# A hybrid-heads encoder kernel: one pipeline for the D, A, B and C attention groups, issued on TensorE in written order, with the attention constants loaded at the start

## The chip, the cores and the metric

The kernel runs on one core of a Trainium2 chip. The metric is the device time of one execution in microseconds (us). The time before is the median of 3 runs, 3581.33 us (3578.38 to 3583.49). PE is TensorE, the matmul engine, and PEld its weight loads; DVE is VectorE, ACT ScalarE, POOL GpSimd, and SP the queue that issues most DMAs.

## The reference

Two layers of an encoder trunk work on 2048 tokens of 1024 channels in float32. A layer is a normalisation, one input projection whose columns belong to four groups of attention heads, a SiLU gate on each group's output, one output projection and a residual add.

```python
for l in range(DEPTH):                      # 2 layers
    z = rmsnorm(x, norm_g[l]) @ w_in[l]     # q, k, v, gate of A, B, C, D
    o_a = dense attention, 4 query heads on 2 key heads, q and k normalised, rotary
    o_b = sliding window of 128 to each side, rotary, a sink logit in the softmax
    o_c = 2-D neighbourhood (8 x 16) with a relative position bias
    o_d = (softmax(q1 k1) - lam * softmax(q2 k2)) @ v, then a norm   # dense, head halves of 32
    x = x + concat(o_a * silu(g_a), ..., o_d * silu(g_d)) @ w_out[l]
out = rmsnorm(x, final_g)
```

lam is a scalar of the layer, made from four small vectors; the sink is one number for each head of B.

## The kernel before

Tokens are handled in 16 tiles of 128. Projections are done with a split of each operand into two float32r parts (three matmuls for each product); scores and outputs of the attention run in float32r or as float32 transposes. A layer goes through four stages.

**1. Projection of D.** For each tile, x is transposed and split (`make_ht`), the D columns are projected, and queries and keys are rotated, transposed and stored. Half of the transposed tiles stay in SBUF, the others go to DRAM.

**2. The D phase.** 32 units (2 key heads x 16 query tiles). A unit computes four passes of scores, 2048 keys each, in four matmuls of 512 columns (L490); DVE moves every score bank to SBUF and takes its maximum (L491); ACT makes the exponential of 2048 columns (L498); DVE combines the two softmaxes of a head (`comb`, L715). Then come eight *fronts*: four 128 x 128 transposes into one PSUM bank (L507) and an evacuation by `evac` (L468 on ACT or L466 on DVE, chosen by the unit's list `ev`, which is empty for D: ACT). Then the *O block*: 32 matmuls with the values (L514). Then the finish `fin_d`, a generator that is advanced once a slot: evacuation, squares, a small matmul (L584), a reciprocal root on POOL (L114), the gate on POOL (L538), a transpose (L543) and the product (L546), which is stored.

Beside it runs the *filler*: the input projection of groups A, B and C, 20 chunks of 8 tiles, each tile (`z`, L315 to L319) 24 matmuls of 256 columns into a PSUM buffer of the pool `zps2` (two buffers), followed by its post-processing. Query chunks (A, B and C: 48 of the 160 tiles) later call `q_store` or `qc_store`, which transpose the finished queries into a `zps2` buffer as well (L754, L798) and evacuate with ACT and DVE (L757, L758); they are called from inside a later tile, after its sixth of eight k steps (`KQ = 5`). In a query chunk of A the rotation and the norm are on POOL (L745, L329, L337, L114, L748).

**3. The A, B and C phase.** 32 groups of three units: one dense A unit and two B units, and in the second half two C units instead. Queries, keys and bias tables are loaded by `prep`; small key tables are built by `k_build` from inside the loop.

**4. Output projection** (L218), during which the next layer's D weights are loaded.

The order in stages 2 and 3 is written out by `drive`. It walks the units; beside a unit's fronts (and, in D, two gap slots ahead of them) it advances the generator of the *next* unit's scores, so that they end with the last front; a *slot* is one such step, and each slot also advances the filler by `FR2 = 12.2` matmuls. Ahead of the first unit it gives half that to each of its 16 score steps.

What this order means differs. Before, the D phase's `drive` call is a plain program: the framework's scheduler takes the written order as a priority, and orders each engine's instructions by its own model of time, so PE may be given a later filler where an earlier instruction isn't ready in that model. Only stage 3's call lies in `tc.manual_schedule(engines={PE})`, where PE's instructions stay in the order in which they are written. On the other engines the scheduler sets the order in both. Between the two calls the pools of stage 2 are closed, the rest of the filler is written out, and stage 3's first loads and first key build are made.

`layer_consts` loads a layer's small tensors, among them `snk` (the sinks), `nsnk` (their negative, by DVE) and `nlam`; the tiles lie in a pool with one buffer, so layer 1's load of a tile waits for layer 0's last reader. It is called once for each layer, ahead of stage 1's loop.

`build_rep` makes C's bias table in DRAM, with POOL copies in a pool of its own (`bb`). It is called by the filler at its seventh chunk.

Of the kernel before, what the change touches and what calls it, by code (L numbers as in the profile page):

```python
# [20 lines left out]
S = 2048  # L21
# [52 lines left out]
def trunk_kernel(ctx, tc, x, norm_g, w_in, w_out, qn_a, kn_a, sink_b, rpb_c, lam_q1, lam_k1, lam_q2, lam_k2,  # L74
# [44 lines left out]
    def build_rep(l, pool):  # L119
        rep = dr.tile([64, 60, 40], F32, name=f"rep{l}")  # L120
        rr = pool.tile([60, 31], F32, name="rraw")
        nc.sync.dma_start(out=rr, in_=rpb_c[l].rearrange("h a b -> (h a) b"))
        G.tensor_scalar(rr, rr, 8.0, 0.0, op0=ALU.mult, op1=ALU.add)
        rint = pool.tile([60, 64], F32, name="rint")
# [7 lines left out]
        for c0, n in ((0, 4), (4, 4), (57, 4), (61, 3)):  # L132
            re = pool.tile([60, 4, 40], F32, tag="redge", name="redge")
# [120 lines left out]

    for l in range(depth):
# [5 lines left out]
        snk = lay.tile([128, 4], F32, tag="snk", name="snk")  # L261
        nsnk = lay.tile([128, 4], F32, tag="nsnk", name="nsnk")
# [4 lines left out]
        nlam = lay.tile([128, 1], F32, tag="nlam", name="nlam")  # L267

        def layer_consts():
# [4 lines left out]
            nc.sync.dma_start(out=snk, in_=sink_b[l].partition_broadcast(128))  # L274
            V.tensor_scalar(nsnk, snk, -1.0, 0.0, op0=ALU.mult, op1=ALU.add)
            for i, a in enumerate((lam_q1, lam_q2, lam_k1, lam_k2)):
                nc.sync.dma_start(out=lv[:, i, :], in_=a[l].partition_broadcast(128))
            V.tensor_tensor(lp, lv[:, 0:2, :], lv[:, 2:4, :], op=ALU.mult)
            V.tensor_reduce(ls, lp, axis=AX.X, op=ALU.add)
            A.activation(le, ls, ACTF.Exp)  # L280
            V.tensor_tensor(nlam, le[:, 1:2], le[:, 0:1], op=ALU.subtract)
            V.tensor_scalar(nlam, nlam, lam_init, 0.0, op0=ALU.subtract, op1=ALU.add)
# [65 lines left out]
        with tc.tile_pool(name="wd", bufs=16, reuse_waits="tile") as wp, tc.tile_pool(name="st", bufs=3, reuse_waits="tile") as st:  # L348
# [107 lines left out]
        with tc.tile_pool(name="sm", bufs=6, reuse_waits="tile") as sm, \  # L456
# [60 lines left out]
            def small_front(u, i):  # L517
                ws, n, kw = u["ws"], u["n"], u.get("kw", 128)
                js = [j for j in (2 * i, 2 * i + 1) if j < n]
                if i == 0:  # L520
                    u["pt"] = u["ptp"].tile([128, 1024], F32, tag="pt", name="PT")
# [55 lines left out]
            def fin_d(u):  # L577
# [3 lines left out]
                yield  # L581
                yield
# [9 lines left out]
                yield  # L592
                yield
                yield
# [124 lines left out]
            with tc.tile_pool(name="st2", bufs=5, reuse_waits="tile") as st, tc.tile_pool(name="w2", bufs=10, reuse_waits="tile") as wp, \  # L719
                    tc.tile_pool(name="z2", bufs=2, reuse_waits="tile") as zp, tc.tile_pool(name="zps2", bufs=2, space=PSUM, reuse_waits="tile") as zps:  # L720
# [129 lines left out]
                def filler():  # L850
# [46 lines left out]
                with tc.tile_pool(name="bb", bufs=1, reuse_waits="tile") as bbp, tc.tile_pool(name="p1", bufs=1, reuse_waits="tile") as p1p:  # L897
                    kds = {(0, 0): kd0[0], (0, 1): kd0[1]}

                    def get_kd(kv):  # L900
                        def f(c):
                            if (kv, c) not in kds:
# [6 lines left out]
                                  p1=p1p, fixed=False, front=dense_front, back=dense_back, get_o=own_o,  # L909
# [283 lines left out]
```

## Time and profile before

| | us |
|---|---|
| median of 3 runs | 3581.33 |
| lowest, highest | 3578.38, 3583.49 |
| the profiled execution | 3577.66 |
| its span, first to last instruction | 3575.9 |
| PE busy in it | 3440.1 |
| DVE busy | 2501.2 |
| ACT busy | 2111.0 |
| POOL busy | 954.5 |
| D phase of layer 0, first score to last O block | 178.4 to 1081 |
| D phase of layer 1 | 1949.6 to 2856 |
| first A O block, layer 0 and 1 | 1095.9 and 2872.9 |

A row of a windows table gives a stretch in us from the span's start and its length, then for each engine the busy time and the number of instructions, the clock that PE was granted as a share of full speed, the share of the DMA engines and GB/s. A row of the timeline gives start and duration, the engine, the line, the operation with its output and inputs, shape and count, and in brackets how long the engine stood idle before it and what ended that. Matmuls are pipelined, so their busy times overlap: how fast PE goes is seen in the distance of starts, or in the number of matmuls in a stretch, not in busy time. A few matmul records are missing or lie on a window's edge, so counts are off by one or two.

### The profile page before, as it was taken

How to read it: one execution, taken by the hardware profiler on the slowest of the kernel's cores; microseconds unless marked ns; L12 is line 12 of the kernel's file. 1: busy time of each engine (PE TensorE's matmuls, PEld its weight loads, DVE VectorE, ACT ScalarE, POOL GpSimd, SP SyncE). 2: the span in 40 equal slices, each digit the busy share in tenths (PEclk: the TensorE clock that was granted, in tenths of full speed). 3: DMA queues.
4: the chain of work that ended last, by engine and by line, in shares of the span. 5: the costliest groups of instructions: out<-in, count | busy, mean ns of one | idle time of the engine just before them, and what ended most of it. 6: DMA issues, size and time to landing. Idle time of an engine off the chain costs nothing. (4 is left out here: it accounts for less than half of the span.)

```text
span 3575.9 us, 71599 instructions
## 1 busy us (share of the span) xinstructions
PE 3440.1 (96%) x25232; PEld 2967.9 (83%) x25232; DVE 2501.2 (70%) x7827; ACT 2111.0 (59%) x3963; POOL 954.5 (27%) x1604
## 2 busy tenths in 40 slices
PE   8989999999989999999999899999999899999999
PEld 8979898888967877877899798988889578778787
DVE  4387877777877887773233878787787778777733
ACT  4455666556667877771144556665666678777711
POOL 4455333552200001001044553256431000010000
PEclk9999999999999999999999999999999999999999
DMA  4542325332233354335445323253331332543243
GB/s 147 187 113 86 79 84 163 93 93 77 70 93 87 83 126 123 90 99 174 146 130 183 99 79 91 70 179 90 81 86 58 96 85 85 136 114 98 89 159 112
DMA packets 355777, 387.47 MB, mean 108 GB/s; under 512 B 59802, under 2 KB 298586, under 8 KB 350298
## 3 DMA queue, kind: packets, MB, share of 16 engines
q1 hardware_dynamic: 351098, 367.17, 35.3%
q10 hardware_dynamic: 4320, 15.73, 1.3%
q8 instruction: 199, 3.26, 0.4%
q14 instruction: 160, 1.31, 0.1%
HBM read 258.83 MB, written 123.91 MB: 107 GB/s over the span
## 5 line engine op out<-in xcount | busy, mean ns | idle before, releaser
L491 DVE TENSOR_SCALAR_CACHE_REDUCE P<-S 128x512 f32<-128x512 f32 x1536 | 1025.6, 685 | 263.6 <-PE S L490 195.2
L315 PE MATMUL z<-wt,ht 128*128 128x256 f32 (+1 forms) x3008 | 890.8, 297 | 8.9 <-ACT wt L306 4.2
L317 PE MATMUL z<-wt,ht 128*128 128x256 f32 (+1 forms) x3008 | 883.8, 294 | 2.7 <-DVE wt L309 2.7
L319 PE MATMUL z<-wt,ht 128*128 128x256 f32 (+1 forms) x3008 | 882.9, 294 | 0.0
L507 PE MATMUL PTp<-idr,P 128*128 128x128 f32 x4096 | 627.5, 276 | 40.9 <-ACT P L468 18.5
L468 ACT COPY P<-PTp 128x512 f32<-128x512 f32 x896 | 511.4, 585 | 220.0 <-PE PTp L507 215.7
L498 ACT ACTIVATE P<-P,nm 128x2048 f32<-128x2048 f32 x256 | 513.9, 2008 | 182.7 <-DVE jk L497 173.9
L507 PEld LDWEIGHTS PTp<-idr,P 128*128 128x128 f32 x4096 | 491.2, 142 | 139.0 <-ACT P L468 25.7
L315 PEld LDWEIGHTS z<-wt,ht 128*128 128x128 f32 x3008 | 569.0, 190 | 28.0 <-POOL wt L308 5.0
L317 PEld LDWEIGHTS z<-wt,ht 128*128 128x128 f32 x3008 | 569.4, 189 | 16.9 <-DVE wt L309 5.2
L319 PEld LDWEIGHTS z<-wt,ht 128*128 128x128 f32 x3008 | 569.2, 189 | 7.0
L490 PE MATMUL S<-kA,q 128*128 128x512 f32 x1024 | 362.7, 437 | 0.0
L218 PE MATMUL y<-wot,ms 128*128 128x512 f32 x1440 | 330.8, 392 | 0.0
L218 PEld LDWEIGHTS y<-wot,ms 128*128 128x128 f32 x1440 | 270.8, 188 | 59.7
L538 POOL TENSOR_TENSOR gg<-gt,rzh 128x128 f32<-128x128 f32 x192 | 76.8, 401 | 894.9 <-PE O L543 351.6
L308 POOL TENSOR_SCALAR wt<-wst,g 128x256 fp32r<-128x256 f32 (+1 forms) x336 | 213.8, 647 | 355.8 <-PE z L319 261.8
L715 DVE SCALAR_TENSOR_TENSOR P<-P,cf,P 128x2048 f32<-128x2048 f32 x128 | 306.4, 2394 | 2.7
L498 ACT ACTIVATE P<-P,nm,rr_a 128x2048 f32<-128x2048 f32 x128 | 268.5, 2098 | 63.1 <-DVE jk L497 60.7
L514 PE MATMUL O<-P,vd 128*64 128x256 f32 x2048 | 242.6, 389 | 0.6 <-ACT P L468 0.6
L514 PE MATMUL O<-P,vA 128*64 128x256 f32 x2048 | 235.1, 382 | 0.0
L490 PE MATMUL S<-kdt,qd 128*128 128x512 f32 x512 | 214.6, 440 | 8.2 <-DVE P L491 5.4
L490 PE MATMUL S<-kd,qd 128*128 128x512 f32 x512 | 208.8, 429 | 12.5 <-DVE P L491 10.9
(195 smaller groups left out, 5120.5 us busy)
## 6 DMA issues: line engine op xcount, KB each, us to landing
wst<-in_w_in_dram SPq DMA_DIRECT2D x320, 128.0 KB
qd<-qd SPq DMA_DIRECT2D x128, 128.0 KB
htd<-ht SPq DMA_DIRECT2D x16, 1024.0 KB
ht<-htd SPq DMA_DIRECT2D x16, 1024.0 KB
q<-qsA SPq DMA_DIRECT2D x128, 128.0 KB
q<-qsB SPq DMA_DIRECT2D x64, 256.0 KB
q<-qc SPq DMA_DIRECT2D x64, 256.0 KB
mload<-mx ACTq DMA_DIRECT2D x30, 512.0 KB
```

What stands on the lines that cost most here:

```text
L218: PE.matmul(ys[c], lhsT=ms[:, a, kc], rhs=wts[k][:, b, c * 512:(c + 1) * 512], start=(k == 0 and i == 0), stop=(k == KD - 1 and i == 2))
L308: G.tensor_scalar(wt[:, 0, :], s, g8[:, k:k + 1], 0.0, op0=ALU.mult, op1=ALU.add)
L315: PE.matmul(z, lhsT=h[:, 0, kc], rhs=wk[:, 0, :], start=(k == 0), stop=False)
L317: PE.matmul(z, lhsT=h[:, 0, kc], rhs=wk[:, 1, :], start=False, stop=False)
L319: PE.matmul(z, lhsT=h[:, 1, kc], rhs=wk[:, 0, :], start=False, stop=(k == KD - 1))
L468: A.copy(dst, src)
L490: PE.matmul(s, lhsT=q, rhs=k_ap[:, c:c + 512], start=(i == 0), stop=(i == len(q_list) - 1))
L491: V.tensor_scalar(p[:, c:c + 512], s, 1.0, None, op0=ALU.mult, op1=ALU.max, accum_out=mx[:, j:j + 1])
L498: A.activation(p, p, ACTF.Exp, bias=nm, scale=scale, accum_out=zacc)
L507: PE.transpose(tp[:, (h * 2 + a) * 128:(h * 2 + a + 1) * 128], p[:, h, j * 128:(j + 1) * 128], idn)
L514: PE.matmul(u["o"][a * 64:(a + 1) * 64, 0:256], lhsT=u["v"](0, j), rhs=u["p"][:, :, j * 128:(j + 1) * 128], start=(n < 2), stop=(n >= NT - 2))
L715: V.scalar_tensor_tensor(p0, p1, cf, p0, op0=ALU.mult, op1=ALU.add)
```

## The change

Both `drive` calls become one, over the 32 D units and the 32 groups of A, B and C, inside one `manual_schedule` for PE: the D phase is now also issued on PE in written order, filler included. The first A unit's scores are preceded by `switch`, which writes out what is left of the filler, closes stage 2's pools, opens stage 3's and makes its first loads; three empty steps follow it. So the first A, B scores are written beside the last D unit's fronts. The first key build of B becomes one of the queued builds, run in the last D unit. The last two D units take their finish's buffer from the same pool as the others, and wait three and five slots in place of two and three. The gap is a property of a unit.

The sink and lam constants of both layers get tiles of their own and are made by `attn_consts`, called once, in layer 0, behind `layer_consts`. `build_rep` gets one buffer out of the rotation of the query chunks (`qs`, three buffers) in place of its own pool, and puts its three tables in parts of it.

"Evacuations by slot" in the change's name has no line of its own in the diff: the lists `ev` are as before.

```diff
-    def build_rep(l, pool):
+    def build_rep(l, buf):
-        rr = pool.tile([60, 31], F32, name="rraw")
+        rr = buf[0:60, 0:31]
-        rint = pool.tile([60, 64], F32, name="rint")
+        rint = buf[0:60, 32:96]
-            re = pool.tile([60, 4, 40], F32, tag="redge", name="redge")
+            re = buf[0:60, 96:256].rearrange("p (c e) -> p c e", e=40)
...
+    snks = [const.tile([128, 4], F32, name=f"snk{m}") for m in range(depth)]
+    nsnks = [const.tile([128, 4], F32, name=f"nsnk{m}") for m in range(depth)]
+    nlams = [const.tile([128, 1], F32, name=f"nlam{m}") for m in range(depth)]
...
-            nc.sync.dma_start(out=snk, in_=sink_b[l].partition_broadcast(128))
-            V.tensor_scalar(nsnk, snk, -1.0, 0.0, op0=ALU.mult, op1=ALU.add)
...
+        def attn_consts():
+            for m in range(depth):
+                nc.sync.dma_start(out=snks[m], in_=sink_b[m].partition_broadcast(128))
+                V.tensor_scalar(nsnks[m], snks[m], -1.0, 0.0, op0=ALU.mult, op1=ALU.add)
+                for i, a in enumerate((lam_q1, lam_q2, lam_k1, lam_k2)):
+                    nc.sync.dma_start(out=lv[:, i, :], in_=a[m].partition_broadcast(128))
+                V.tensor_tensor(lp, lv[:, 0:2, :], lv[:, 2:4, :], op=ALU.mult)
+                V.tensor_reduce(ls, lp, axis=AX.X, op=ALU.add)
+                A.activation(le, ls, ACTF.Exp)
...
             if l == 0:
                 load_wd()
                 layer_consts()
+                attn_consts()
                 nc.sync.dma_start(out=bm, in_=bmask)
...
-            def drive(groups, gap, fill, f_rate, extra=None):
+            def drive(groups, fill, f_rate, extra):
                 fins = []
+                k3 = len(units_d)
...
+                    gap = g[0].get("gap", 0)
...
-                            if extra:
-                                extra(step[0])
-                            step[0] += 1
+                            if k >= k3 - 1:
+                                extra(step[0] if k >= k3 else f - 10)
+                            if k >= k3:
+                                step[0] += 1
...
                         if i == 6:
-                            build_rep(l, bbp)
+                            build_rep(l, zp.tile([128, 256], F32, tag="qs", name="rbuf", bufs=3))
...
                     for u in units[-2:]:
-                        u["fp"] = lambda: zps.tile([128, 256], F32, tag="z", name="fin")
-                    drive([[u] for u in units], GAP2, fill, FR2)
-                for _ in fill:
-                    pass
-                for f in pend_all:
-                    f()
-                for _ in side:
-                    pass
+                        u["f1"], u["f2"] = 3, 5
+                    units_d = [[u] for u in units]
...
+            def switch():
+                nonlocal tpool
+                for _ in fill:
+                    pass
+                for f in pend_all:
+                    f()
+                for _ in side:
+                    pass
+                flush()
+                ph2.close()
+                for nm, bufs in (("qst", 2), ("ql", 2), ("cb", 1), ("px", 4), ("pt", 2)):
+                    X[nm] = ph3.enter_context(tc.tile_pool(name=nm, bufs=bufs, reuse_waits="tile"))
+                for nm in ("ops2", "tps3"):
+                    X[nm] = ph3.enter_context(tc.tile_pool(name=nm, bufs=1, space=PSUM, reuse_waits="tile"))
+                tpool = cycle([tps, tps, X["tps3"]])
+                bint[1] = X["cb"].tile([128, 4, 480], F32, name="bint1")
+                cm["pool"] = X["cb"]
+                prep(0, 0)
+                kt["B"] = [big.tile([128, S], F32R, tag="b", name=f"kB{i}") for i in range(2)]
+                builds.extend(("B", 0, [e]) for e in k_load(X["ql"], "B", 0))
                 load_v("A")
-                kt["B"] = [big.tile([128, S], F32R, tag="b", name=f"kB{i}") for i in range(2)]
-                k_build("B", 0, k_load(ql, "B", 0))
                 load_v("B")
...
+                def a_first(u):
+                    switch()
+                    for _ in range(3):
+                        yield
+                    yield from a_scores(u)
...
-                with tc.manual_schedule(engines={mybir.EngineType.PE}):
-                    drive([units[i:i + 3] for i in range(0, len(units), 3)], GAP3, iter(()), 0, ex3)
+                first = units[0]
+                first["ns"] += 3
+                first["s"] = a_first
+                order = ExitStack()
+                order.enter_context(tc.manual_schedule(engines={mybir.EngineType.PE}))
+                drive(units_d + [units[i:i + 3] for i in range(0, len(units), 3)], fill, FR2, ex3)
+                order.close()
+                ph3.close()
```

More of the change, by code (lines that the diff above doesn't have):

```diff
@@ L260, in trunk_kernel @@
         sub = lay.tile([128, 64], F32, tag="sub", name="sub")
-        snk = lay.tile([128, 4], F32, tag="snk", name="snk")
-        nsnk = lay.tile([128, 4], F32, tag="nsnk", name="nsnk")
+        snk, nsnk, nlam = snks[l], nsnks[l], nlams[l]
         lv = lay.tile([128, 4, 32], F32, tag="lv", name="lv")
@@ L266, in trunk_kernel @@
         le = lay.tile([128, 2], F32, tag="le", name="le")
-        nlam = lay.tile([128, 1], F32, tag="nlam", name="nlam")
         def layer_consts():
@@ L273, in layer_consts @@
             G.tensor_scalar(sub, sub, 0.5 * (1.0 - lam_init), 0.0, op0=ALU.mult, op1=ALU.add)
[L274 to L282, printed above, removed]
+        def attn_consts():
[7 more added lines that the diff above has]
+                A.activation(le, ls, ACTF.Exp)
+                V.tensor_tensor(nlams[m], le[:, 1:2], le[:, 0:1], op=ALU.subtract)
+                V.tensor_scalar(nlams[m], nlams[m], 0.8 - 0.6 * math.exp(-0.3 * m), 0.0, op0=ALU.subtract, op1=ALU.add)
         if l > 0:
@@ L580, in fin_d @@
                 A.activation(sq, os, ACTF.Square)
-                yield
-                yield
+                for _ in range(u.get("f1", 2)):
+                    yield
                 tp = u["fp"]()
@@ L591, in fin_d @@
                 gg = finish(u["g"], rr)
-                yield
-                yield
-                yield
+                for _ in range(u.get("f2", 3)):
+                    yield
                 finish2(gg, os, u["t"], u["fb"], u["o"], u["fp"])
@@ L717, in d_scores @@
                     yield
-            with tc.tile_pool(name="st2", bufs=5, reuse_waits="tile") as st, tc.tile_pool(name="w2", bufs=10, reuse_waits="tile") as wp, \
-                    tc.tile_pool(name="z2", bufs=2, reuse_waits="tile") as zp, tc.tile_pool(name="zps2", bufs=2, space=PSUM, reuse_waits="tile") as zps:
+            if True:
+                ph2 = ExitStack()
+                st = ph2.enter_context(tc.tile_pool(name="st2", bufs=5, reuse_waits="tile"))
+                wp = ph2.enter_context(tc.tile_pool(name="w2", bufs=10, reuse_waits="tile"))
+                zp = ph2.enter_context(tc.tile_pool(name="z2", bufs=2, reuse_waits="tile"))
+                zps = ph2.enter_context(tc.tile_pool(name="zps2", bufs=2, space=PSUM, reuse_waits="tile"))
                 def sumsq_heads(z, rs, H):
@@ L896, in trunk_kernel @@
                 fill = filler()
-                with tc.tile_pool(name="bb", bufs=1, reuse_waits="tile") as bbp, tc.tile_pool(name="p1", bufs=1, reuse_waits="tile") as p1p:
+                p1p = ph2.enter_context(tc.tile_pool(name="p1", bufs=1, reuse_waits="tile"))
+                if True:
                     kds = {(0, 0): kd0[0], (0, 1): kd0[1]}
@@ L1058, in pair_o @@
                 if u["kv"] == 0:
-                    o_bc.append(ops2.tile([128, 512], F32, tag="o", name="Obc"))
+                    o_bc.append(X["ops2"].tile([128, 512], F32, tag="o", name="Obc"))
                 u["o"] = o_bc[-1]
             o_bc = []
-            def small_unit(sc, i, t, q, px, fb, ns, nv, bias=None, pre=lambda: None):
-                return dict(kv=i, t=t, s=sc, par=False, ev=(0, 1) if i else (), ns=ns, nv=nv, fin=fin_plain, fb=fb, q=q, pp=px, bias=bias, pre=pre,
-                            front=small_front, back=small_back, get_o=pair_o, oc=128 * i, ptp=ptp, fd=5 + 2 * i)
@@ L1068, in trunk_kernel, with small_unit @@
-            with tc.tile_pool(name="qst", bufs=2, reuse_waits="tile") as qst, tc.tile_pool(name="ql", bufs=2, reuse_waits="tile") as ql, \
-                    tc.tile_pool(name="cb", bufs=1, reuse_waits="tile") as cb, tc.tile_pool(name="px", bufs=4, reuse_waits="tile") as px, \
-                    tc.tile_pool(name="pt", bufs=2, reuse_waits="tile") as ptp, \
-                    tc.tile_pool(name="ops2", bufs=1, space=PSUM, reuse_waits="tile") as ops2, \
-                    tc.tile_pool(name="tps3", bufs=1, space=PSUM, reuse_waits="tile") as tps3:
-                tpool = cycle([tps, tps, tps3])
+            def small_unit(sc, i, t, q, fb, ns, nv, bias=None, pre=lambda: None):
+                return dict(kv=i, t=t, s=sc, par=False, ev=(0, 1) if i else (), ns=ns, nv=nv, fin=fin_plain, fb=fb, q=q, bias=bias, pre=pre,
+                            front=small_front, back=small_back, get_o=pair_o, oc=128 * i, fd=5 + 2 * i)
@@ new lines, in trunk_kernel @@
+            X, ph3 = {}, ExitStack()
+            loaded, builds = [], []
+            bint = [None, None]
+            cc_, edge = {}, {}
+            cm, qq = {}, {}
+            def switch():
[18 more added lines that the diff above has]
+                builds.extend(("B", 0, [e]) for e in k_load(X["ql"], "B", 0))
@@ L1074, in trunk_kernel @@
                 load_v("A")
[L1075 to L1076 removed]
                 load_v("B")
[L1078 to L1082 removed]
+            if True:
                 def prep(ps, t):
@@ L1146, in ex3 @@
                         k_build(*builds.pop(0))
-                    if step == WOU:
+                    if step == WOU and not wo_tiles:
                         for k in range(KD):
```

33 lines of the change are left out of this document (14 added, 19 removed).

## The prediction

> **What bounds the kernel now.** I read the page's first part, then a table of windows by stage, then the same kind of table for single units of the D phase, then the timeline where TensorE (PE) stands still.
>
> ```profile
> span 3575.9 us, 71599 instructions
> PE 3440.1 (96%) x25232; PEld 2967.9 (83%) x25232; DVE 2501.2 (70%) x7827; ACT 2111.0 (59%) x3963; POOL 954.5 (27%) x1604
> ```
>
> PE is busy for 96% of the span, but busy time is not speed: the windows by stage show how many matmuls it gets through. For layer 0 they are the start of the D phase (178 to 236), the stretch with filler (236 to 1008) and the stretch after the filler has run out (1008 to 1096); the last two again for layer 1.
>
> ```profile
> core 0: us, PE busy (x) PEld busy (x) DVE busy (x) ACT busy (x) POOL busy (x), PEclk, DMA share, GB/s
> 178.00:236.00 58.00, 46.72 (x299) 41.77 (x301) 49.34 (x142) 28.14 (x49) 46.67 (x81) 0.88 0.49 128
> 236.00:1008.00 772.00, 762.53 (x6006) 686.74 (x6003) 606.03 (x1829) 465.35 (x807) 296.12 (x490) 1.00 0.32 91
> 1008.00:1096.00 88.00, 69.43 (x407) 46.52 (x407) 68.63 (x241) 58.54 (x95) 9.04 (x15) 0.94 0.37 102
> 2009.00:2782.00 773.00, 764.24 (x6007) 688.47 (x6007) 606.48 (x1829) 465.34 (x807) 294.98 (x491) 1.00 0.32 91
> 2782.00:2873.00 91.00, 74.84 (x407) 49.47 (x407) 69.05 (x241) 58.62 (x95) 9.04 (x15) 0.89 0.35 98
> ```
>
> With filler PE does 6006 matmuls in 772 us, 7.8 a microsecond, and waits 9.5 us in all. After the filler it does 407 in 88 us, 4.6 a microsecond, in both layers. There VectorE (DVE) and ScalarE (ACT) set the pace, through a chain of waits. So PE bounds the filled part, the other two the tail, and where the filler ends matters.
>
> The next two tables hold windows from one unit's O block to the next, first for the filler line L319 alone (a third of the filler), then for everything.
>
> ```profile
> 830.72:855.22 24.50, 9.21 (x33) 6.21 (x33) 1.00 0.34 91
> 969.78:1000.01 30.23, 14.96 (x54) 9.99 (x53) 1.00 0.18 49
> 1000.01:1019.22 19.21, 3.08 (x11) 2.07 (x11) 1.00 0.52 137
> ```
>
> ```profile
> 830.72:855.22 24.50, 24.16 (x187) 21.06 (x186) 21.51 (x67) 15.03 (x30) 6.84 (x14) 1.00 0.34 91
> 969.78:1000.01 30.23, 30.23 (x245) 27.97 (x244) 23.30 (x68) 18.87 (x33) 3.84 (x7) 1.00 0.18 49
> 1019.22:1039.08 19.86, 14.92 (x83) 8.61 (x82) 16.58 (x54) 13.16 (x19) 1.10 (x2) 1.00 0.45 99
> 1039.08:1060.77 21.69, 17.43 (x87) 11.57 (x86) 18.30 (x59) 13.16 (x19) 1.10 (x2) 0.81 0.23 73
> 2793.24:2814.46 21.22, 17.16 (x83) 10.83 (x82) 16.91 (x54) 13.20 (x19) 1.10 (x2) 0.83 0.38 82
> 2814.46:2834.68 20.22, 16.86 (x87) 9.83 (x86) 17.58 (x58) 13.26 (x19) 1.10 (x2) 0.92 0.23 73
> ```
>
> A unit with 33 x 3 = 99 fillers takes 24.50 us, one with 54 x 3 = 162 takes 30.23: 0.091 us for each more. The scheduler gives out filler unevenly and ahead of the written rate, and three units and three quarters of a fourth are left nearly without.
>
> **Part 1: filler at its written rate.** The written order spends 98 fillers beside unit 0's scores and 122 (10 slots of 12.2) beside each unit's fronts. 3840 (160 tiles of 24) last for (3840 - 98) / 122 = 30.67 of 32 units, so 1.33 stay without, against 3.74 now (the windows after 1019.22, 1039.08 and 1060.77, and 1 - 33/122 of the one at 1000.01). A unit with 122 fillers takes 24.50 + 23 x 0.091 = 26.6 us. What PE needs for it without them comes from the pace of issue:
>
> ```profile
> 982.07 0.60 PE L507 MATMUL PTp<-idr,P 128*128 128x128 f32 x4
> 982.42 0.47 PE L490 MATMUL S<-kdt,qd 128*128 128x512 f32 x1
> 982.73 0.28 PE L319 MATMUL z<-wt,ht 128*128 128x256 f32 x1
> 982.85 0.28 PE L315 MATMUL z<-wt,ht 128*128 128x256 f32 x1
> ```
>
> Start to start a filler takes 0.12 us, four transposes 0.35, a score about 0.3 behind a transpose. 26.6 - 122 x 0.12 = 12.0 us. The four unfilled units above took 20.75 us on average, so each wastes 8.75. With 2.4 fewer in each layer the change removes 2.4 x 8.75 = 21 us, 42 in both. Moving filler between filled units is free, as their pace is linear. The scores of the first A unit lie beside the tail in both orders.
>
> **Part 2: constants.** In layer 0, where group B ends and C begins:
>
> ```profile
> 1335.57 4.00 SPq L274 DMA_DIRECT2D snk<-in_sink_b_dram  x1
> ```
>
> ```profile
> 1347.28 0.17 DVE L275 TENSOR_SCALAR nsnk<-snk 128x4 f32<-128x4 f32 x1 [9.14 <-DMA snk<-in_sink_b_dram]
> ```
>
> ```profile
> 1348.11 0.97 PE L1036 MATMUL Sc<-kC,q 128*128 128x360 f32 x2 [7.99 <-DVE P L491]
> ```
>
> Layer 1's nsnk is queued on DVE behind a load that could not start before layer 0 had read the old snk; DVE stands 9.14 us, PE 7.99 behind it. With a tile for each layer, loaded at the start, this wait goes: -8. What is late next there is PE's own work; I take nothing back. In exchange one more load chain and its DVE steps lie in the opening. The second lv set is read early in the program already, so what is new is snk, nsnk and nlam of one layer. Between 0 and one more DMA wait; DVE waited 1.88 us on the first snk:
>
> ```profile
> 21.48 0.17 DVE L275 TENSOR_SCALAR nsnk<-snk 128x4 f32<-128x4 f32 x1 [1.88 <-DMA snk<-in_sink_b_dram]
> ```
>
> I take 2.
>
> **Part 3: waits that the written order adds.** PE can no longer step past an instruction that isn't ready; behind it queue every score, transpose and filler, and DVE and ACT wait for those. Most steps have cover: the stretch of A and B units, issued in written order already, lost 0.31 us of 50 and then 0.76.
>
> ```profile
> 1100.00:1150.00 50.00, 49.69 (x411) 40.24 (x406) 41.02 (x156) 40.26 (x89) 3.60 (x9) 1.00 0.30 83
> 1150.00:1200.00 50.00, 49.24 (x405) 40.11 (x404) 41.65 (x156) 40.33 (x85) 3.61 (x9) 1.00 0.35 93
> ```
>
> That is 1% or less, as the filled stretch loses now, so I charge nothing for it. One step has little cover. The input-projection tiles z and the transposed queries qT share two PSUM buffers. In a query chunk (48 of 160 tiles) qT is transposed six fillers before the tile's end, and the next tile takes the buffer that ACT (L757) and DVE (L758) must have emptied, or z's own. The cover is six fillers and about one score: 6 x 0.12 + 0.4 = 1.1 us. I paired the 66 transposes on record with the DVE subtraction that ends each. The shortest pair, the middle one and a long one:
>
> ```profile
> 361.81 0.38 PE L754 MATMUL qT<-idr,qs 128*128 128x128 f32 x2
> 397.11 0.38 PE L754 MATMUL qT<-idr,qs 128*128 128x128 f32 x2
> 390.15 0.38 PE L754 MATMUL qT<-idr,qs 128*128 128x128 f32 x2
> ```
>
> ```profile
> 362.64 0.42 DVE L758 TENSOR_TENSOR qt<-qT,qt 128x256 fp32r<-128x256 f32 x1 [0.65 <-ACT qt L757]
> 399.33 0.40 DVE L758 TENSOR_TENSOR qt<-qT,qt 128x256 fp32r<-128x256 f32 x1
> 395.07 0.41 DVE L758 TENSOR_TENSOR qt<-qT,qt 128x256 fp32r<-128x256 f32 x1
> ```
>
> They hold the buffer for 1.25, 2.62 and 5.33 us: 0.15 us uncovered at the short end, 1.5 in the middle. About 80 tiles of both layers meet this in the steady part (the first eight of a layer lie in the start). 12 us or 120: I take 0.3 us a tile, 24 in all, nearer the short end, because a waiting PE sends no new scores and both engines empty their queues, and because z's own buffer is a second way out.
>
> In the start, PE waits now for POOL's query chain, and POOL for weights:
>
> ```profile
> 201.07 0.69 PE L754 MATMUL qT<-idr,qs 128*128 128x128 f32 x2 [4.90 <-POOL qs L748]
> ```
>
> ```profile
> 188.65 0.48 POOL L308 TENSOR_SCALAR wt<-wst,g 128x256 fp32r<-128x256 f32 x1 [5.36 <-DMA wst<-in_w_in_dram]
> ```
>
> The written order meets tile 0's last weights after 24 fillers and four scores, where the scheduler ran tile 1's filler instead: up to 5 us worse in a layer. build_rep now takes its buffer from the query rotation, so its POOL steps and loads leave this stretch: up to 4 us better. I take 0. The query and key loads at the switch are issued, as now, right after the last filler, with the unfilled third of a unit, an O block and two slots as cover; without it one load's wait would show, once in a layer.
>
> **The sum.** Against the profiled execution, 3577.66 us (span 3575.9): -42 - 8 + 2 + 24 = -24, so 3554. The median of the three runs, 3581.33, lies 3.7 above that execution; on the median's footing I forecast 3557. A difference of 0.2%, 7 us, is about what a measurement of this kernel can tell from none.
>
> **A page weighed.** In the window at 1039.08 the granted clock is 0.81, and PE's longest wait there is:
>
> ```profile
> 1045.55 0.44 PE L507 MATMUL PTp<-idr,P 128*128 128x128 f32 x2 [1.91 <-DVE P L715]
> ```
>
> The Trainium skill, "TensorE: Matmul & The Clock Gate", section "Part 1: The HAM clock gate", lets the clock fall only after an idle window of about 3.4 us; by it new waits of 0.3 or 1.5 us cost themselves alone. The trace does not agree: waits under 2 us came with 0.81. If the 80 query tiles, 5.2 us each (26.6 x 24/122), ran at 0.81, that would add 80 x 5.2 x 0.19 = 79 us. I leave it out of the sum, as the A and B stretch with its short waits shows 1.00, and keep it for the upper end.
>
> **Rivals.** *Slower: the shared PSUM buffers decide.* If the middle pair holds, 80 x 1.5 = 120 us are lost against 48 gained: +72, 3653 on the median's footing. It decides from 0.6 us a tile (48 / 80). For it: the middle and the long pairs, and DVE and ACT are busy for 79% and 60% of the filled stretch. Against it: the short pairs, and the scheduler's order itself kept running through these chunks.
>
> *No change: the first front waits.* Front 0 needs the combination of both heads, and in written order it comes two slots after the O block, 24.4 x 0.12 + 3.2 x 0.3 = 3.9 us. One of the late ones:
>
> ```profile
> 803.86 3.67 PE L514 MATMUL O<-P,vd 128*64 128x256 f32 x32
> ```
>
> ```profile
> 808.84 2.35 DVE L715 SCALAR_TENSOR_TENSOR P<-P,cf,P 128x2048 f32<-128x2048 f32 x1
> ```
>
> The block's issue ends 3.6 us after its start, the combination 3.7 us later: just covered. If DVE is 0.4 us later in each of some 60 units, 24 us go and with them the gain: about 3581. For this case also speaks that "evacuations by slot" has no line in the diff: the lists that choose DVE or ACT are the same, so that part does nothing.
>
> *Better still:* if the 9.5 and 8.8 us that PE waits in the filled stretches go too and the query tiles cost 0.15, the sum is -54, 3527.
>
> **How the numbers follow.** The forecast's case, 3535 to 3574: 0.53. Better still: 0.05. No change: 0.15. Slower: 0.27. So faster 0.58, same 0.15, slower 0.27. The range runs from 3515 to 3610; above it lie query tiles that cost over about 0.95 us each, roughly half of the slower case.
>
> **What would show it.** Right: 122 fillers in every D window but the last two, D units at 26 to 27 us, filler lasting to about 30 us before the last D block, no wait at nsnk, and the C phase and output projection unchanged. Wrong: PE waits at L315 behind ACT L757, L739 or DVE L758 summing to over 24 us a layer, waits at L507 behind L715, or D units of 28 us with 122 fillers.

## The result, and the profile after

| | time, us | against before |
|---|---|---|
| before | 3579.86, median of 4 runs (3576.71 to 3583.49) | |
| after | 3638.76, median of 4 runs (3633.92 to 3641.12) | 1.0158, 95% interval 1.0145 to 1.0171 |

The change makes the kernel 59 us slower by the medians, 57 by the ratio; the forecast was 3557, at most 3610. The first lines of the page of the changed kernel:

```profile
span 3632.1 us, 71548 instructions
PE 3431.5 (94%) x25232; PEld 2980.2 (82%) x25232; DVE 2508.2 (69%) x7827; ACT 2127.3 (59%) x3963; POOL 928.8 (26%) x1604
```

The span grew by 56.2 us, and PE's busy time fell by 8.6: the work is the same, the waiting grew. To see where, the D phase of layer 0 of the changed kernel from O block to O block, as in the prediction (columns: window, its length, then busy time and instructions of each engine, PE's clock, the DMA engines' share, GB/s). A unit without queries, three with query chunks (groups B, B and C), and the last two units:

```profile
core 0: us, PE busy (x) PEld busy (x) DVE busy (x) ACT busy (x) POOL busy (x), PEclk, DMA share, GB/s
272.40:298.50 26.10, 26.10 (x209) 23.65 (x207) 21.75 (x67) 16.01 (x27) 8.31 (x16) 1.00 0.27 77
378.10:409.70 31.60, 28.22 (x218) 24.99 (x217) 20.75 (x63) 17.62 (x30) 15.63 (x26) 1.00 0.26 65
409.70:441.80 32.10, 28.24 (x216) 24.93 (x215) 24.52 (x70) 17.69 (x32) 8.52 (x13) 1.00 0.30 80
441.80:481.60 39.80, 29.21 (x218) 25.40 (x217) 23.73 (x73) 17.62 (x35) 11.00 (x31) 0.98 0.36 88
...
1069.40:1092.40 23.00, 21.89 (x167) 18.92 (x166) 18.05 (x55) 14.14 (x25) 1.10 (x2) 1.00 0.23 80
1092.40:1113.20 20.80, 14.96 (x95) 11.35 (x95) 14.94 (x54) 14.63 (x22) 3.65 (x4) 0.92 1.06 275
```

All 29 units between the start and the last two hold 122 fillers. Those without queries take 25.9 to 27.9 us and PE stands 1.5 us in them at most; the last two are the only short ones, as forecast. Of the nine with query tiles, the two that hold B's second query chunk take only 27.3 and 27.9 us; the other seven take 30.8 to 39.8 us, and PE stands 3.4, 3.9 and 10.6 us in the three shown. What PE waits for, in the changed kernel's waits (engine, line and who ended the wait: us in all, times, longest):

```profile
PE z L320 <- DVE qt L770: 20.4, 22, 1.7
...
PE z L320 <- ACT qs L802: 13.9, 18, 1.5
PE z L320 <- POOL wt L313: 13.8, 4, 5.8
...
PE PTp L513 <- DVE P L723: 11.7, 4, 3.7
...
PE z L320 <- ACT zkv L778: 10.9, 8, 2.5
PE qT L810 <- DVE qc L819: 10.2, 4, 3.5
...
PE z L320 <- ACT zq L751: 8.9, 12, 1.2
PE z L320 <- ACT sq L736: 7.6, 5, 2.3
```

L320 is a tile's first projection matmul (L315 before). It waits for the buffer that the previous qT held (DVE qt) and for the one that the previous z held (ACT qs, zkv, zq, sq). L810 is the transposing of C's queries into their own qT. These six rows sum to 72 us in both layers. The prediction had named two of them as the sign that it is wrong, DVE qt and ACT zq (L758 and L739 before), above 24 us a layer: these two come to 29 us in both layers, so that sign by itself didn't show, while its other one, D units above 28 us with 122 fillers, did. The whole stretch from the first D score to the first A unit's O block took 917.5 and 923.3 us before in the two layers and takes 942.8 and 950.5 after, so +52.5 in all. The first D score itself comes 5.8 us later (184.2 against 178.4), and the stretch from the first A unit's O block to the first C score is 5.8 shorter (246.4 against 252.2).

### The profile page after: what moved, and what is told of

Same layout as the page of the kernel before. It is cut to its first block, busy times and chain, and to the rows that moved or that the text cites. A ratio compares the mean times of both kernels' runs of the same rounds, so it can differ in the third digit from the quotient of the medians.

```text
span 3632.1 us, 71548 instructions
## 1 busy us (share of the span) xinstructions
PE 3431.5 (94%) x25232; PEld 2980.2 (82%) x25232; DVE 2508.2 (69%) x7827; ACT 2127.3 (59%) x3963; POOL 928.8 (26%) x1604
## 4 chain that ended last, share of the span: by engine, by line
PE 74%; DVE 10%; DMA 5%; issue 4%; ACT 4%; POOL 2%; SPq 1%; POOLq 0%; DVEq 0%; ACTq 0%
PE S L496 10%; PE O L520 10%; PE y L218 10%; PE PTp L513 10%; PE z L320 9%; PE z L322 8%; PE z L324 8%; DVE P L497 4%; PE Obc L539 2%; PE PTp L531 2%; DVE P L723 2%; ACT P L504 2%; DMA wst<-in_w_in_dram 2%; PE Sc L1043 1%; DVE wt L314 1%
## 5 line engine op out<-in xcount | busy, mean ns | idle before, releaser
L497 DVE TENSOR_SCALAR_CACHE_REDUCE P<-S 128x512 f32<-128x512 f32 x1536 | 1038.6, 686 | 226.4 <-PE S L496 219.2
L320 PE MATMUL z<-wt,ht 128*128 128x256 f32 (+1 forms) x3008 | 896.8, 298 | 80.5 <-DVE qt L770 14.1
L474 ACT COPY P<-PTp 128x512 f32<-128x512 f32 x896 | 520.6, 585 | 351.7 <-PE PTp L513 347.2
L320 PEld LDWEIGHTS z<-wt,ht 128*128 128x128 f32 x3008 | 569.9, 189 | 112.5 <-ACT qs L802 19.3
L313 POOL TENSOR_SCALAR wt<-wst,g 128x256 fp32r<-128x256 f32 (+1 forms) x336 | 195.1, 591 | 450.7 <-PE z L324 332.4
L496 PE MATMUL S<-kdt,qd 128*128 128x512 f32 x512 | 229.3, 448 | 11.6 <-DVE P L497 11.4
L496 PE MATMUL S<-kd,qd 128*128 128x512 f32 x512 | 228.2, 446 | 4.5 <-DVE P L497 4.5
```

The source lines that it names most:

```text
L313: G.tensor_scalar(wt[:, 0, :], s, g8[:, k:k + 1], 0.0, op0=ALU.mult, op1=ALU.add)
L320: PE.matmul(z, lhsT=h[:, 0, kc], rhs=wk[:, 0, :], start=(k == 0), stop=False)
L474: A.copy(dst, src)
L496: PE.matmul(s, lhsT=q, rhs=k_ap[:, c:c + 512], start=(i == 0), stop=(i == len(q_list) - 1))
L497: V.tensor_scalar(p[:, c:c + 512], s, 1.0, None, op0=ALU.mult, op1=ALU.max, accum_out=mx[:, j:j + 1])
```

## Experiments

Theory: the written order turns the two PSUM buffers that z and qT share into waits. Rivals: the constants, the merged pipeline, or DVE and ACT being late whatever the buffers. Ratios are to the kernel before on the same chip. A difference of two ratios is multiplied by 3582 to give us; by the two intervals such a difference is uncertain by 5 to 8 us.

| run | median us | ratio, 95% interval |
|---|---|---|
| e6_order | 3635.72 | 1.0149 (1.0134 to 1.0164) |
| e3_noorder | 3581.65 | 0.9999 (0.9989 to 1.0008) |
| e2_consts | 3585.32 | 1.0010 (1.0000 to 1.0019) |
| e1_half | 3592.21 | 1.0028 (1.0017 to 1.0040) |
| e7_side | 3584.72 | 1.0000 (0.9991 to 1.0010) |
| e8_casts | 3551.93 | 0.9908 (0.9893 to 0.9923) |
| e9_late | 3548.76 | 0.9899 (0.9884 to 0.9914) |
| e10_nolate | 3569.89 | 0.9956 (0.9941 to 0.9971) |
| f1_aftercasts | 3612.66 | 1.0083 (1.0067 to 1.0100) |
| f2_beforecasts | 3591.02 | 1.0025 (1.0015 to 1.0035) |
| f3_actw | 3539.96 | 0.9881 (0.9866 to 0.9895) |
| f4_actstart | 3536.27 | 0.9866 (0.9850 to 0.9883) |
| g1_twotiles | 3568.39 | 0.9970 (0.9955 to 0.9984) |
| g2_mendnoorder | 3576.24 | 0.9988 (0.9979 to 0.9998) |

### Which part of the change

**e6_order**: the kernel before, and only this:

```
+                    with tc.manual_schedule(engines={mybir.EngineType.PE}):
                         drive([[u] for u in units], GAP2, fill, FR2)
```

> The kernel before with the written order on PE in D alone; two drives, old constants, old buffers. Theory (the written order in D is the whole loss): query units of 31 to 40 us as in the changed kernel, filler to the last unit but one, 3630 to 3660. Rival (the order brings the gain of the tail and something else in the change loses it): below 3570.

1.0149, nearly the whole change. The same three query units, in the windows of this run:

```profile
373.70:405.30 31.60, 28.24 (x216) 24.98 (x215) 20.77 (x63) 17.58 (x30) 15.17 (x25) 1.00 0.28 65
405.30:437.50 32.20, 28.31 (x218) 24.98 (x217) 24.55 (x70) 17.79 (x32) 8.56 (x13) 1.00 0.32 81
437.50:473.60 36.10, 28.64 (x220) 25.11 (x219) 23.69 (x73) 18.16 (x35) 6.83 (x14) 1.00 0.32 86
```

31.6 and 32.2 us are the changed kernel's own, the third is 3.7 shorter. **e3_noorder** is the counterpart: the changed kernel, its written order entered at the switch.

```
                     switch()
+                    order.enter_context(tc.manual_schedule(engines={mybir.EngineType.PE}))
...
                 order = ExitStack()
-                order.enter_context(tc.manual_schedule(engines={mybir.EngineType.PE}))
```

> The changed kernel, with the written order on PE beginning only at the switch to the A units, as before the change; one pipeline, constants and buffers stay as changed. Theory (the written order in D is the whole loss): 3570 to 3585, as the kernel before with its constants moved. Rival (the merged pipeline, its longer-lived pools and the rebuilt query buffer cost time): above 3600.

0.9999. So the pipeline, the moved buffers and the constants together cost nothing that this run shows; the order on PE in D is the loss. **e2_consts**: the kernel before with the constants alone.

```
-        nsnk = lay.tile([128, 4], F32, tag="nsnk", name="nsnk")
+        snk, nsnk, nlam = snks[l], nsnks[l], nlams[l]
...
                 layer_consts()
+                attn_consts()
```

> The kernel before with the constants part alone. Theory: the 8 us wait at layer 1's nsnk between groups B and C of layer 0 goes, the opening gets some 5 us longer by the ten more loads ahead of the next x tile, so 3 us better, 3577, hardly to be told from none. Rival (a part of the loss is the constants): 3590 or more.

1.0010, 3.6 us and no gain: between the theory's 3577 and the rival's 3590. First A O block to first C score takes 243.9 us in place of 252.2, but the first D score comes at 184.1, and in the profiled execution, the longest of the ten, layer 0's stretch from the first D score to the first A O block takes 931.3 us in place of 917.5, though nothing in D was edited. In the changed kernel the queue of SP shows why the opening is longer (its issues there, then the same x load in the kernel before):

```profile
22.97 0.42 SPq L279 DMA_DIRECT2D snk<-in_sink_b_dram  x1
25.46 0.80 SPq L282 DMA_DIRECT2D lv<-in_lam_q_dram  x2
26.32 0.90 SPq L282 DMA_DIRECT2D lv<-in_lam_k_dram  x2
...
27.73 0.43 SPq L379 DMA_DIRECT2D xt<-in_x_dram  x1
```

```profile
23.58 0.42 SPq L374 DMA_DIRECT2D xt<-in_x_dram  x1
```

The second layer's snk and four lv loads stand ahead of the x tile's; before, that load was issued at 23.58, so 4.2 us are lost. PE then waits for it:

```profile
34.59 3.68 PE L168 MATMUL xT<-idr,xt 128*128 128x128 f32 x16 [4.76 <-DMA xt<-in_x_dram]
```

### Why the query units are long

**e1_half**: qT goes into the free half of the z tile's own PSUM buffer, at the tile's end, so that z alone alternates between the two buffers.

```
-                    p = zps.tile([128, 256], F32, tag="z", name="qT")
+                    p = (zps.tile([128, 512], F32, tag="z", name="qT") if zz is None else zz)[:, 256:512]
...
-                                if k == KQ and len(pend) > 1:
-                                    pend.pop(0)()
+                                if k == KD - 1 and len(pend) > 1:
+                                    pend.pop(0)(zz)
```

> The changed kernel, but qT no longer takes a PSUM buffer of its own: it is transposed at the end of an input-projection tile into the free half of that tile's buffer, so the two z buffers simply alternate. Theory (the shared buffers are the loss): the query units fall from 31 to 40 us towards the 26 us of the others, some 45 of the 60 us a layer above that come back, and the time is 3535 to 3575. Rival (in written order the query units are long for another reason, the evacuations of scores and fronts queued behind the query work on ACT and DVE): the query units stay above 30 us and the time above 3615.

1.0028: 46.6 us of the 56.6 come back (1.0158 - 1.0028 = 0.0130). The edit frees the buffer and also moves the transposes from the sixth to the eighth k step; what each is worth isn't separated. The theory gets the larger part right, but 3592 is above its 3575, and three units a layer stay long (C's first query chunk; A's second; C's second with the first transposes of A's keys, kT0; e1_half):

```profile
430.00:464.70 34.70, 29.34 (x216) 26.77 (x216) 23.07 (x73) 18.28 (x35) 8.99 (x18) 0.90 0.38 96
...
651.90:686.40 34.50, 29.33 (x216) 26.12 (x216) 29.18 (x87) 19.08 (x35) 27.85 (x38) 0.95 0.36 95
...
879.20:915.90 36.70, 30.45 (x216) 26.96 (x216) 23.63 (x70) 15.95 (x33) 8.20 (x18) 0.86 0.30 81
```

Each holds one long wait, and now the clock is below 1.00. **e7_side** puts kT0's transposes into the half buffer too, at a tile's end.

```
-                        p = zps.tile([128, 512], F32, tag="z", name="kT0")[:, 0:256]
+                        p = half[0][:, 256:512]
```

> As e1_half, and the transposes of group A's first keys (kT0) also go into the free half of a z tile's buffer, at a tile's end, in place of a buffer of their own. In e1_half the wait of such a transpose for ACT's evacuation of zkv, 6.2 us, stands in a D unit of 36.7 us where its neighbours take 28. Theory (what is left of the loss is a few long waits for shared buffers, each with a slow clock behind it): that unit falls to 28 us in both layers, 17 us in all, 3568 to 3583. Rival (DVE and ACT are that far behind in this unit whatever the buffers): the wait moves to the next z and the time stays at 3588 to 3596.

1.0000, 10 us. Between the two: the unit fell from 36.7 to 32.3 us, not to 28; a wait of 3.8 us moved to the next z, as the rival said. **e8_casts** changes the order of four instructions in group C's query evacuation:

```
                     for x in range(2):
-                        A.copy(hi, px)
-                        V.tensor_tensor(lo, px, hi.bitcast(F32), op=ALU.subtract)
+                        A.copy(hi[:, x], px[:, x])
+                    for x in range(2):
+                        V.tensor_tensor(lo[:, x], px[:, x], hi[:, x].bitcast(F32), op=ALU.subtract)
```

> As e7_side, and in the evacuation of group C's queries ACT makes both casts before DVE makes both subtractions, so that ACT no longer waits for DVE between them. In e1_half that wait was 4.4 us once, and PE waited 5.36 for the query evacuation behind it. Theory (ACT is held by DVE's backlog there): the units of 29, 35 and 31 us fall to 27 or 28, 10 to 14 us a layer, 3545 to 3562. Rival (DVE's backlog itself is the limit, the wait for the subtraction only moves to the buffer's release): less than 8 us below e7_side.

0.9908, 33 us, inside the theory's range and more than the 20 to 28 that it counted. In e7_side, DVE, ACT and PE at the end of layer 0's first C query chunk, one after the other:

```profile
451.44 2.57 DVE L723 SCALAR_TENSOR_TENSOR P<-P,cf,P 128x2048 f32<-128x2048 f32 x1
454.94 0.48 DVE L819 TENSOR_TENSOR qc<-z,qc 128x128 fp32r<-128x128 f32 x2
```

```profile
455.25 0.27 ACT L818 CAST qc<-z 128x128 fp32r<-128x128 f32 x1 [4.81 <-DVE qc L819]
455.45 0.47 ACT L802 ACTIVATE qs<-z,rstd 128x256 f32<-128x256 f32 x1
```

```profile
455.98 0.58 PE L320 MATMUL z<-wt,ht 128*128 128x256 f32 x1 [5.77 <-ACT qs L802]
```

DVE is busy with the scores' combination of 2.57 us and comes to the first subtraction at 454.94; ACT stands 4.81 us for it before its second cast; behind that cast is the evacuation (L802) that PE waits for, 5.77 us. In e8_casts the same stretch on ACT:

```profile
449.50 0.43 ACT L818 CAST qc<-z 128x128 fp32r<-128x128 f32 x2 [0.58 <-PE z L810]
449.82 0.49 ACT L802 ACTIVATE qs<-z,rstd 128x256 f32<-128x256 f32 x1
455.05 0.47 ACT L802 ACTIVATE qs<-z,rstd 128x256 f32<-128x256 f32 x1 [0.44 <-DVE qc L820]
```

The evacuation that came at 455.45 comes at 449.82. DVE is as late as before (454.54), but PE stands behind it only 0.55 us. **g1_twotiles** asks what made ACT wait: as e7_side, with qc as two tiles in SBUF.

```
-                        hi, lo = qt[:, x, :, 0, r0:r0 + 2, :], qt[:, x, :, 1, r0:r0 + 2, :]
+                        hi, lo = qt[x][:, :, 0, r0:r0 + 2, :], qt[x][:, :, 1, r0:r0 + 2, :]
```

> As e7_side (cast, subtraction, cast, subtraction in group C's query evacuation), but the two halves of qc are two tiles in SBUF, with four store DMAs of half the size in place of two. Theory A (ACT waits for DVE between the casts because both read the same PSUM bank, as every handover of a bank between two engines is ordered): nothing gained, 3577 to 3590, with the wait of the second cast for DVE's subtraction still there. Theory B (the wait comes from the shared SBUF tile): as e8_casts, 3548 to 3558.

0.9970, between the two: neither theory's time. The rows decide for the bank as far as the wait goes. ACT in g1_twotiles:

```profile
451.82 0.27 ACT L818 CAST qc<-z 128x128 fp32r<-128x128 f32 x1
452.44 0.27 ACT L818 CAST qc<-z 128x128 fp32r<-128x128 f32 x1 [0.36 <-PE z L810]
456.36 0.47 ACT L802 ACTIVATE qs<-z,rstd 128x256 f32<-128x256 f32 x1 [3.65 <-DVE qc L819]
```

ACT still stops for DVE, and the longest stop is now L802's own: it reads z from the PSUM buffer whose other half DVE's subtraction reads, and shares no SBUF tile with it. The Trainium skill, "PSUM — Partial Sum Buffer", section "PSUM bank collisions raise a hardware error", says that two engines' accesses to one bank have to be kept apart by the software even when both only read; these rows agree. The two tiles still brought 11 us (1.0000 - 0.9970); whether by the shared tile's part in the wait or by the order on ACT, which differs too, isn't separated.

**f1_aftercasts** and **f2_beforecasts** make e8's edit alone, in the changed kernel and in the kernel before.

> The changed kernel with only the two casts ahead of the two subtractions in group C's query evacuation; qT keeps its own PSUM buffers. Theory (shared buffers and ACT's wait for DVE are two causes that add up): some 30 below the changed kernel, 3600 to 3615, with the group B and A query units still at 31 to 35 us. Rival (ACT's wait for DVE is the one cause, and the shared buffers only pass it on): 3560 or less.

> The kernel before with only the two casts ahead of the two subtractions. Theory (the scheduler's order steps past a tile whose evacuation is late, so the wait costs it little): 3570 to 3582, less than 10 us of gain. Rival (the edit would help any order alike, and what e8_casts gained says nothing of the written order): 3545 to 3560.

The first gives 1.0083, 27 us better than the changed kernel, its B query units unchanged at 31.6 and 32.2 us and the C unit down from 39.8 to 32.6: two causes that add up. What holds ACT in the changed kernel is, however, less the subtraction itself (5.5 us in all, 0.8 at most) than what follows from it: qc has one buffer, and its store has to be done before the next pair of tiles is cast. DVE, SP and ACT of the changed kernel, then the store in f1_aftercasts:

```profile
470.01 0.28 DVE L819 TENSOR_TENSOR qc<-qT,qc 128x128 fp32r<-128x128 f32 x1
475.05 1.21 SPq L822 DMA_DIRECT2D qc<-qc  x2
479.29 0.27 ACT L818 CAST qc<-qT 128x128 fp32r<-128x128 f32 x1 [4.91 <-DMA qc<-qc]
```

```profile
465.64 1.62 SPq L823 DMA_DIRECT2D qc<-qc  x2
```

The second subtraction comes behind a combination of 2.46 us, the store after that behind transfers of build_rep, and ACT's next cast stands 4.91 us for the store; PE's wait of 3.09 us at 480.83 follows from it. In f1_aftercasts both subtractions come before the combination, and the store is issued 9.4 us earlier.

The second gives 1.0025, 9 us slower, outside the ranges of theory and rival: with the scheduler's order the edit brings no gain, and D's order changes with it (917.5 and 923.3 us from the first score to the first A block become 926.2 and 927.9). ACT's stops at these casts are alike in the kernel before and the changed one (5.7 and 5.5 us behind the subtraction, 15.8 and 16.3 behind the store). But PE's waits in the kernel before have no row of a tile's first matmul behind ACT qs, zkv, zq or DVE qt. So ACT's waits were always in the kernel; the written order made them count on PE.

**f3_actw**: in e8_casts the longest wait left behind the start is PE's for POOL's query sum at the end of an A query chunk (3.9 and 5.0 us, units of 35.5). Eight weights of the next chunk are then scaled on ACT, not POOL (with e9_late, below, as its base).

```
-  wnext.append(load_w(wp, st, len(wnext), nxt[0][1], 256))
+  wnext.append(load_w(wp, st, len(wnext), nxt[0][1], 256, i in (0, 10)))
```

> As e9_late, and the eight weights that are prepared at the end of group A's two query chunks are scaled on ACT, not on POOL. In e8_casts POOL works through the query chunk without a pause, its eight scalings push the last query tile's sum back, and PE waits 3.9 and 5.0 us for it in units of 35.5 us. Theory (POOL's backlog is the last long wait): these units fall to 28 us, 14 us in both layers, 3530 to 3540. Rival (ACT, with eight scalings of some 0.5 us more, keeps the evacuations waiting instead): within 5 us of e9_late, with waits behind ACT zq.

0.9881, 6 us below e9_late, less than the 14 expected and hardly told from none, though 3540 is at the edge of what the theory gave: the unit falls from 34.2 to 29.3 us in layer 0 and from 34.8 to 31.1 in layer 1, and PE's waits have no row for POOL's query sum any more. **f4_actstart** scales the start's last four weights on ACT too.

```
-  load_w(wp, st, k, plan[0][0][1], 256) for k in range(len(wpre), KD)
+  load_w(wp, st, k, plan[0][0][1], 256, True) for k in range(len(wpre), KD)
```

> As f3_actw, and the last four of the first chunk's weights are scaled on ACT too, at the start of D, where PE waits 5.5 us for POOL's scaling of a weight in each layer. Theory (POOL is late there with queries and weights): 3 to 5 us a layer, the first O block comes 53 us after the first score in place of 57.5, 3522 to 3535. Rival (that scaling waits for its load): no difference from f3_actw, and the wait stands behind ACT.

The rival holds: the start stays at 58.1 us, and ACT, too, waits for the loads (first row, behind which PE stands 5.23 us; the second sums such waits of PE in f4_actstart):

```profile
186.77 0.51 ACT L311 ACTIVATE wt<-wst,g 128x256 fp32r<-128x256 f32 x1 [1.24 <-DMA wst<-in_w_in_dram]
```

```profile
PE z L320 <- ACT wt L311: 15.7, 3, 6.2
```

Its 0.9866 isn't told from f3_actw's. One of its four runs took 9759 us; it is counted in the median of the table (the median of the other three is 3533.86), not in the ratio, and nothing here explains it.

### What the written order is worth

**g2_mendnoorder**: f4_actstart with the scheduler's order in D, by e3_noorder's edit.

> As f4_actstart with all its mends, but the written order on PE begins only at the switch to the A units, so that the scheduler orders the D phase. Theory (once its waits are mended the written order is worth the 42 us that its filler rate promised, less what the mends help the scheduler): 3565 to 3585, 30 to 45 above f4_actstart. Rival (the mends help any order and the written order is worth nothing): 3530 to 3545.

0.9988 against 0.9866: 44 us, where the forecast had 42 for the filler's rate. The fastest kernel with the scheduler's order in D is e10_nolate below, without the mends, at 0.9956; against it the written order is worth 32 us. D of layer 0, before first, then f4_actstart, each from its first score to the start of its last O block:

```profile
178.40:1077.40 899.00, 862.73 (x6597) 762.82 (x6595) 710.52 (x2154) 541.13 (x926) 349.67 (x580) 0.99 0.34 95
```

```profile
177.60:1062.40 884.80, 849.81 (x6605) 767.96 (x6603) 710.52 (x2166) 554.00 (x948) 331.22 (x560) 0.99 0.34 97
```

For the changed kernel this window is 929.0 us. From the first D score to the first A O block f4_actstart takes 901.4 and 897.8 us in the two layers, 41.6 less in all than the kernel before. **e9_late** and **e10_nolate** move the constants' loads beside the fifth tile, in e8_casts and in e3_noorder.

```
-                attn_consts()
...
+                if l == 0 and t == 4:
+                    attn_consts()
```

> As e8_casts, with the loads of the constants (snk, nsnk, nlam of both layers) issued four tiles later, beside the fifth tile of the first stage, instead of ahead of the second x tile's load. Theory (these ten loads ahead of the x tile are the 5.5 us by which the first D score came later): first D score at 178 to 179 us, 5 to 6 us below e8_casts. Rival (they cost the same wherever they are): first D score stays at 183 to 184.

> As e3_noorder (scheduler's order in D), with the constants' loads four tiles later. Theory: 5 to 6 us below e3_noorder, 3574 to 3577: the gain at nsnk is then kept. Rival (the scheduler's order of D varies with any edit by 10 us or more, as from e2_consts to the kernel before): anything from 3568 to 3590, with the first D score at 178 all the same.

The first D score comes at 179.6 and 178.1 us in place of 184.3 and 183.9, as the theory said but for 0.6 us. e9_late gains 3.2 us of those 4.7, which isn't told from none. e10_nolate gains 15, of which the opening is 5.8; the first-score-to-A stretches are 3.0 and 7.3 us shorter, so here the rival (the scheduler's order varies with any edit) holds too.

## Why the prediction was wrong

**Filler at its written rate: right.** 122 in each unit, 25.9 to 27.9 us without queries (26.6 forecast), the last two units at 23.0 and 20.8, and 44 us from the order once it is mended (42). That the two numbers are so close is in part luck: against e10_nolate it is 32.

**Constants: right in kind, +2 mis-sized.** The wait goes, worth 5.8 (8 forecast), but the opening costs 5.8: the working counted one wait on the first snk, and took the second lv set as read early already; in the kernel before it was loaded behind the x tile, and now five loads more stand ahead of that tile in one queue.

**The 0.3 us a query tile is the step that failed.** The mends brought 46.6 (e1_half), 10.0 (e7_side), 33.0 (e8_casts) and 6.4 (f3_actw): 96 us. About 11 of it belong to the start (61.9 and 64.2 us against 57.7 and 57.3 in e8_casts) and 10 to the transposes of A's first keys, which the prediction took at 0 or didn't price. The other 75 are 0.9 us for each of the 80 query tiles, where 0.3, 24 in all, was taken. The bounds, 0.15 and 1.5, held it, and 0.6 was the point from which the slower rival decides; the wrong end was chosen. Nor is it one price a tile: PE stands 1.4 us in the two units with B's second chunk, 10.6 in the one unit of C's first. The two reasons given for the short end were both wrong:
- "A waiting PE sends no new scores and both engines empty their queues": DVE's queue at a chunk's end holds a combination of 2.6 us and the eight weights of the next chunk, and they don't wait for PE. In e7_side DVE was busy without a break while PE stood 5.77 us.
- "z's own buffer is a second way out": L320 waited for it (ACT qs, zkv, zq, sq) 41 us in all, against 20 for qT's.

A third thing wasn't looked at: the 66 pairs were all of groups A and B (L754). Group C's evacuation (L806, L807 before) has four steps that go back and forth between ACT and DVE, and a store behind them, and was priced by the rows of A and B; its order was 33 us of the 96.

**The start: taken at 0, it cost 4.6 us a layer** (61.9 and 64.2 us to the first O block, 57.3 and 59.6 before). That e1_half takes it back (57.0, 56.8) shows that the query transposes did it, by their buffer or their place, not the weights, whose wait for POOL stands in both (13.8 and 14.5 us).

**A and B as witness: right for units without queries only.** That stretch has no query tiles, so it couldn't speak for them.

**The rivals.** The slower one came true in its mechanism, with 0.9 us a tile in place of 1.5, and with group C's handovers, the start and the key transposes besides. The wait of front 0 for the combination showed only 4 times, 11.7 us in all, in each layer's first and last unit.

**The sum by the measured terms:** -44 (order) + 96 (the four mends: query tiles, start and keys) - 5.8 + 5.8 (constants) = +52, against 57 by the ratio; with 32 for the order it is +64. Both lie within the uncertainty of these differences. The terms are steps of one chain of runs, so the sum is no independent check.

## What to carry to other kernels

Before an engine's order is written down, list every buffer on which its next instruction can wait, and price each by what is queued on the releasing engine at the worst moment, not by the shortest hold: here the scheduler's order hid late releases that the fixed one paid for. Read the code of every kind of tile, since one with more handovers between engines may hold a large part, a third of it here. Once the releases were mended, the written order gave 32 to 44 us where its rate promised 42, and f4_actstart, at 0.9866, beats both kernels.

## What the runs showed of the hardware

A long wait of PE costs more than itself. Windows of 1 us of e8_casts round its wait of 3.85 us for POOL's query sum; the clock is the column behind POOL's:

```profile
671.00:672.00 1.00, 0.00 (x0) 0.00 (x0) 1.00 (x5) 0.00 (x0) 1.00 (x2) 0.80 0.00 0
672.00:673.00 1.00, 0.64 (x3) 0.65 (x4) 1.00 (x2) 0.00 (x0) 0.92 (x2) 0.50 0.42 131
...
677.00:678.00 1.00, 1.00 (x6) 1.00 (x6) 0.41 (x2) 1.00 (x1) 0.00 (x0) 0.50 0.00 1
```

Some 6 us at half the clock, by estimate 3 us lost (half of 6), behind 3.85 of waiting. In the changed kernel a wait of 3.09 us brought 0.50 as well; those of 1.86 and 2.21 left 1.00 in every window from 466 to 480:

```profile
470.43 0.41 PE L810 MATMUL qT<-idr,qs 128*128 128x128 f32 x2 [1.86 <-DVE qc L819]
474.43 0.39 PE L320 MATMUL z<-wt,ht 128*128 128x256 f32 x1 [2.21 <-ACT zkv L778]
480.83 0.66 PE L810 MATMUL qT<-idr,qs 128*128 128x128 f32 x2 [3.09 <-DVE qc L819]
```

```profile
480.00:481.00 1.00, 0.17 (x1) 0.20 (x2) 1.00 (x4) 0.66 (x2) 1.00 (x6) 0.69 0.00 0
481.00:482.00 1.00, 1.00 (x5) 0.71 (x6) 0.45 (x4) 0.48 (x1) 0.92 (x4) 0.50 0.04 8
```

The Trainium skill, "TensorE: Matmul & The Clock Gate", section "Part 1: The HAM clock gate", which the prediction weighed, has the clock halve after an idle window of about 3.4 us. The waits of 1.86, 2.21 and 3.85 agree; that of 3.09 doesn't quite: it is shorter, and the mean of 0.69 puts the fall before its end, some 2.6 us into it. The 79 us kept for the upper end didn't come: the query units of the changed kernel ran at 0.95 to 1.00. One place of the kernel before still doesn't agree, the wait of 1.91 us at 1045.55 that the prediction showed (one of 1.81 at 1058.68 in the same tail is followed by 0.50 too); its tail has sparse work on both sides:

```profile
1044.00:1045.00 1.00, 0.00 (x0) 0.00 (x0) 1.00 (x1) 0.00 (x0) 0.00 (x0) 1.00 0.00 0
1045.00:1046.00 1.00, 0.44 (x2) 0.20 (x2) 1.00 (x2) 0.00 (x0) 0.00 (x0) 0.95 0.00 0
1046.00:1047.00 1.00, 0.84 (x2) 0.52 (x2) 0.99 (x6) 0.59 (x1) 0.00 (x0) 0.50 0.00 0
```

What makes the clock fall there stays open.
